# A two-layer mixer trunk on one core: three, and two, of the gate blocks computed beside the keys are handed out around the first attention units

## The chip, the cores and the metric

The kernel runs on one core of one Trainium2 chip. The metric is the time of one execution on the device in microseconds (us), as a median of runs. TensorE is called PE, its weight loads PEld, VectorE DVE, ScalarE ACT, GpSimd POOL and SyncE SP; SP issues all the transfers.

## The reference

Two layers (`DEPTH` = 2) over 1024 latent tokens of 1024 channels with 256 context tokens in front. All weights and activations are float32. Cut to what matters here:

```python
h = _rms(x) * (1.0 + scale) + shift                 # hc for the context tokens
fa, za, u, vs, zb, q, k, va, zc, g = _split_proj(h @ w_in[l])
q = _axial_rope(_qk(q, N_HEADS, q_norm_g[l]), row, col)      # 8 heads of 64
k = _axial_rope(_qk(k, N_KV_HEADS, k_norm_g[l]), row, col)   # 2 key heads
attn = _latent_attn(q, k, va, kc, vc, attn_sink[l])          # window +-128, plus all context keys
ya = _fourier(fa) * silu(za)
yb = _sgu(u, vs, w_s, b_s) * silu(zb)
yc = attn * silu(zc)
ga, gb, gc = split(sigmoid(g), 3)                            # the gates: 3 x 1024 channels
out = (ga * (ya @ w_pa) + gb * (yb @ w_pb) + gc * (yc @ w_pc)) @ w_out
x = x + gate * out
```

In layer 0 the context tokens go through the same (`out_c`), in layer 1 they only give keys and values.

## The kernel before

All matrix products are made of three float32r matmuls each (`mm3`, lines 229 to 231: high x high, high x low, low x high), so a weight tile `raw` is fetched (L209), cast to `whi` on ACT (L212), and the rest `wlo` is made by a subtraction on DVE (L213, called the split here). There are two `raw` buffers and five of `whi` and `wlo`. The tokens stand in three groups, "C" (256 of the context), "0" and "1" (512 latent ones each). A projection with channels on partitions (`proj_cm`) is a chain of 24 matmuls (8 slices of 128 input channels x 3) of 256 or 512 columns into one PSUM bank.

PSUM has eight banks, by tag: two `mm`, three `s`, two `pt`, one `o`. Nearly all chains of projections go into the two `mm` banks: keys and queries, and everything that is computed beside them.

`attention` first makes keys and values, one tile of 128 tokens after the other (the loop over `names`), then goes over the units: two query-head pairs of one token tile (of 128) each, first all tiles of key head 0, then of key head 1. Layer 0 has 40 units, the first four of them those of the context, layer 1 has 32. A unit needs its queries (`queries`, which keeps an `mm` bank from its chain through norm, rotary and transpose to L439), its scores (`scores`: L354 mask, L356, L357 and L363, reduces on DVE, exponentials on ACT, L379 on POOL) and its values (`values`: transposes L391, split on ACT and DVE L260 and L261, matmuls L398 and L399).

Other projections fill PE meanwhile. They are generators that yield the number of columns they have computed; a `Fill` runs them up to a given number. Two sets are used:

- `before_work`, handed out beside the keys as `early`. It computes gate blocks ahead (`ahead`): a block is the tanh of one 128-channel slice j of gate b (0, 1, 2) for one group. In layer 0 it is the first 12 blocks of the context group (`context_blocks(range(12))`), one after each key tile, and the rest at the end (`early.rest()`). In layer 1 it is the blocks (0, 1), (2, 1), (0, 2), (2, 2) of group "0", each in two halves of 256 columns (`part` = CTX), two halves after each key tile of group "1".
- `side_work`, handed out as `fills[0]` in the first half of the units and `fills[1]` in the second. The first yields the silu of the two `Z` and two `A` slices, and the rows `F`; how many columns come with each unit is `S["cost"]` over half the number of units.

The tanh of a gate block (L633) reads the bank and goes into a staging tile, `se` (two buffers of 256 columns) before the units, `st` (three of 512) from then on, and from there to memory (L634); `gates` reads it back much later (L545). A silu is a tanh on ACT (L551) and a multiplication on DVE (L552), which frees the bank.

The code does not fix the order on the engines: the instructions are recorded with `schedule_with_timeline_sim=True`, and the scheduler sorts them by its own estimate within what the dependences allow. A column number in `Fill` thus sets the order in which the instructions are recorded, which the scheduler starts from.

Of the kernel before, what the change touches and what calls it, by code (L numbers as in the profile page):

```python
# [66 lines left out]
def trunk_kernel(ctx: ExitStack, tc: tile.TileContext, a: dict, out: bass.AP):  # L67
# [343 lines left out]
    def attention(l, groups, sideA, sideB, xp, wkv, X, S):  # L411
# [48 lines left out]
        for ig, g in enumerate(names):  # L460
            if ig == 2:
                prepare(0)
                prepare(2)
            if X and ig < 2:
                modulate(l, names[ig + 1], X[names[ig + 1]], xp)
            g0, n = GROUPS[g]
            pk = bank("pt")
            for i in range(n // 128):
                t = g0 // 128 + i
                ib += 1  # L470
                p = bank("mm" if ib % 2 else "s")
                proj_tm(p, wt, H[g], i * 128)
                kf = qk_norm_rope(p, 2, 2, rope, None if g == "C" else t, np_)
                pv = p[:, 128:256].rearrange("p (g d) -> p g d", g=2)

                ACT.mul(vt[:, t, :, 0:64], pv, 0.5)
                DVE.scalar_tensor_tensor(vt[:, t, :, 64:128], pv, 0.5, vt[:, t, :, 0:64].bitcast(F32), ALU.mult, ALU.subtract)
                PE.transpose(pk[:, i * 128:(i + 1) * 128], kf[:, 0:128], ident)
                if "C" in groups:
                    early.upto(early.done + 1)  # L480
                elif ig == 2:
                    early.upto(early.done + CTX + 1)
            for kv in range(2):
                src = pk[kv * 64:(kv + 1) * 64, :n]
                hi = kk[0:64, kv, g0:g0 + n]
                ACT.copy(hi, src)
                DVE.tensor_tensor(kk[64:128, kv, g0:g0 + n], src, hi.bitcast(F32), ALU.subtract)
# [20 lines left out]
        def first(u):  # L508
            kv, g, t, pr = units[u]
            prepare(u)  # L510
            return scores(l, kv, pr, Q[kv, t], kk, local(u), ap)

        cur = first(0)
        nu = len(units)
        for u, (kv, g, t, pr) in enumerate(units):
            if u + 4 < nu:
                prepare(u + 4)
# [48 lines left out]
    def side_work(l, groups, S, st):  # L566

        ntok = sum(GROUPS[g][1] for g in groups)
        S["cost"] = [6 * ntok, 6 * ntok + 14 * CTX * ("C" in groups)]
        for g in groups:  # L570
            for j in range(4):
                stored(S, ("O" if j < 2 else "Z", j, g), GROUPS[g][1])
# [2 lines left out]
        def silus(name, col, js, keep=True):  # L575
            for j in js:
                w = w_cm(l, col + j * 128)
                for g in groups:
                    n = GROUPS[g][1]
                    p = bank("mm")  # L580
                    proj_cm(p, w, H[g], n)
                    s = staged(st, n)
                    silu2(s, p, n)
                    if name == "Y":
                        o = fetched(st, S["O", j, g], n, 2)
                        POOL.tensor_tensor(s, s, o, ALU.mult)
                    nc.sync.dma_start(S[name, j, g] if (name, j, g) in S else stored(S, (name, j, g), n), s)
                    yield n

        def gated_u():  # L590
            for j in range(2):
# [12 lines left out]
                    nc.sync.dma_start(stored(S, ("U", j, g), n), s)  # L604
                    yield 2 * n

        return ([silus("Z", C_ZC, (2, 3)), silus("A", C_ZA, (0, 1))] + [rows(l, groups, "F", C_FA, S, st)],
                [silus("Y", C_ZC, (0, 1)), gated_u()] + ([ahead(l, context_blocks(range(12, 24)), S, st), rows(l, ["C"], "V", C_VS, S, st)] if "C" in groups else []))

    def before_work(l, groups, S, st):  # L610

        if "C" in groups:
            return ahead(l, context_blocks(range(12)), S, st)
        return ahead(l, [(b, j, "0") for j in (1, 2) for b in (0, 2)], S, st, CTX)

    def few(gen, n):
        for _ in range(n):
# [498 lines left out]
```

## Time and profile before

| | before |
|---|---|
| median of 3 runs | 1968.52 us (1967.72 to 2089.09) |
| the profiled execution | 1967.06 us |
| its span, first to last instruction | 1965.3 us |
| PE busy | 1901.6 us, 97% |
| DVE, ACT, POOL busy | 1087.8, 799.5, 627.5 us |
| mean granted clock of PE | 0.994 |

The page's busy time of PE counts a matmul from its start to its modelled end; neighbours overlap, so a chain's length is read from the starts. An idle time stands in brackets behind the instruction that ended it, with the engine and the line that it waited for. The granted clock is 1.00 at 2.4 GHz and 0.50 at 1.2 GHz; a stretch between has both. The keys of layer 0 are made from about 45 to 145 us, its units run to about 500; in layer 1 the keys run to about 1180, the units to about 1490.

### The profile page before, as it was taken

The page shows a single profiled execution, that of the slowest core. Times are in us where ns is not written, and L with a number is a line of the kernel's source. Part 1 is how long each engine was busy: PE and PEld are TensorE (multiplying, and loading weights), DVE is VectorE, ACT ScalarE, POOL GpSimd, SP SyncE. Part 2 cuts the span into 40 slices and gives each one's busy share as a digit, 9 for nine tenths or more (in the row PEclk, how much of TensorE's full clock was granted, in tenths as well). Part 3 has the DMA queues.
Part 4 walks back from the last instruction along what each step waited for, and adds up shares of the span by engine and source line. Part 5 has one row for each costly group of instructions (what it writes and reads, how often), then busy time and mean ns, then how long its engine had stood idle before and what let it go on. Part 6 is the DMA issues. An engine that isn't in the chain of part 4 may idle for free.

```text
span 1965.3 us, 32941 instructions
## 1 busy us (share of the span) xinstructions
PE 1901.6 (97%) x11887; PEld 1688.0 (86%) x11887; DVE 1087.8 (55%) x2211; ACT 799.5 (41%) x2090; POOL 627.5 (32%) x1011
## 2 busy tenths in 40 slices
PE   7989999999999999999999989999999999999999
PEld 2888999999988887888899989899888888888898
DVE  4664665556655648766355455676665655622342
ACT  2653565445644422111243435565554443111320
POOL 1563344533331112211235543344432021211132
PEclk9999999999999999999999999999999999999999
DMA  8431121212565677654464312122134568632462
GB/s 309 119 99 64 50 68 54 79 44 84 163 188 164 188 226 227 171 174 141 148 229 165 108 47 75 54 61 82 34 91 149 158 186 270 191 106 82 134 225 87
DMA packets 281147, 259.91 MB, mean 132 GB/s; under 512 B 20824, under 2 KB 234520, under 8 KB 280984
## 3 DMA queue, kind: packets, MB, share of 16 engines
q1 hardware_dynamic: 280984, 257.80, 41.7%
q8 instruction: 94, 1.54, 0.3%
q14 instruction: 69, 0.57, 0.1%
HBM read 196.91 MB, written 60.83 MB: 131 GB/s over the span
## 4 chain that ended last, share of the span: by engine, by line
PE 82%; DMA 6%; DVE 5%; ACT 3%; issue 2%; POOL 2%; SPq 1%; POOLq 0%; DVEq 0%; ACTq 0%
PE mm L229 16%; PE mm L230 16%; PE mm L231 16%; PE s L230 6%; PE s L229 6%; PE s L231 6%; PE pt L391 3%; PE o L399 2%; PE o L398 2%; PE s L363 1%; PE s L356 1%; DVE wlo L213 1%; DMA raw<-in_w_in_dram 1%; PE s L166 1%; PE s L357 1%
## 5 line engine op out<-in xcount | busy, mean ns | idle before, releaser
L212 ACT CAST whi<-raw 128x1024 fp32r<-128x1024 f32 (+2 forms) x210 | 202.2, 966 | 393.7 <-PE s L230 144.6
L213 DVE TENSOR_TENSOR wlo<-raw,whi 128x1024 fp32r<-128x1024 f32 (+2 forms) x210 | 243.9, 1164 | 213.7 <-ACT whi L212 209.4
L229 PE MATMUL mm<-hh,whi 128*128 128x512 f32 (+1 forms) x768 | 296.2, 386 | 6.6 <-DVE st L552 4.2
L231 PE MATMUL mm<-hh,wlo 128*128 128x512 f32 (+1 forms) x768 | 294.2, 383 | 0.7 <-DVE wlo L213 0.7
L230 PE MATMUL mm<-hl,whi 128*128 128x512 f32 (+1 forms) x768 | 294.4, 383 | 0.0
L229 PE MATMUL mm<-whi,hh 128*128 128x256 f32 x832 | 239.7, 288 | 6.6 <-DVE qt L439 2.5
L231 PE MATMUL mm<-whi,hl 128*128 128x256 f32 x832 | 237.5, 285 | 0.0
L230 PE MATMUL mm<-wlo,hh 128*128 128x256 f32 x832 | 237.3, 285 | 0.0
L674 POOL TENSOR_TENSOR m<-m,tb 128x512 f32<-128x512 f32 x64 | 87.2, 1364 | 409.5 <-DVE tb L673 366.8
L229 PEld LDWEIGHTS mm<-hh,whi 128*128 128x128 f32 x768 | 145.2, 189 | 33.6 <-DVE st L552 5.1
L231 PEld LDWEIGHTS mm<-hh,wlo 128*128 128x128 f32 x768 | 145.1, 189 | 27.7 <-DVE wlo L213 0.9
L229 PEld LDWEIGHTS mm<-whi,hh 128*128 128x128 f32 x832 | 160.3, 193 | 9.0 <-issue 3.1
L230 PEld LDWEIGHTS mm<-hl,whi 128*128 128x128 f32 x768 | 145.3, 189 | 25.3
L231 PEld LDWEIGHTS mm<-whi,hl 128*128 128x128 f32 x832 | 160.5, 193 | 0.2 <-DVE hl L284 0.2
L230 PEld LDWEIGHTS mm<-wlo,hh 128*128 128x128 f32 x832 | 160.4, 193 | 0.2
L379 POOL TENSOR_SCALAR P<-P,rd 128x640 f32<-128x640 f32 (+2 forms) x144 | 110.7, 780 | 105.7 <-DVE rd L377 64.1
L230 PE MATMUL s<-hl,whi 128*128 128x512 f32 x352 | 137.5, 391 | 0.0
L229 PE MATMUL s<-hh,whi 128*128 128x512 f32 x352 | 137.4, 390 | 0.0
L231 PE MATMUL s<-hh,wlo 128*128 128x512 f32 x352 | 137.2, 390 | 0.0
L261 DVE TENSOR_TENSOR pl<-pt,ph 128x512 fp32r<-128x512 f32 (+1 forms) x184 | 112.4, 616 | 39.5 <-ACT ph L260 36.3
L260 ACT CAST ph<-pt 128x512 fp32r<-128x512 f32 (+1 forms) x184 | 96.1, 535 | 32.6 <-PE o L398 18.7
L196 DVE SCALAR_TENSOR_TENSOR aacc<-araw,scol,aacc 128x256 f32<-128x256 f32 x196 | 102.9, 558 | 5.2 <-DMA araw<-in_w_ada_dram 2.8
(303 smaller groups left out, 4637.1 us busy)
## 6 DMA issues: line engine op xcount, KB each, us to landing
raw<-in_w_in_dram SPq DMA_DIRECT2D x122, 512.0 KB, 4.1
araw<-in_w_ada_dram SPq DMA_DIRECT2D x48, 512.0 KB, 6.0
raw<-in_w_out_dram SPq DMA_DIRECT2D x40, 512.0 KB, 3.9
dP<-st SPq DMA_DIRECT2D x64, 256.0 KB, 2.7
lp<-dP SPq DMA_DIRECT2D x64, 256.0 KB, 4.2
x<-in_x_dram SPq DMA_DIRECT2D x16, 512.0 KB, 9.3
raw<-in_w_pc_dram SPq DMA_DIRECT2D x32, 256.0 KB, 2.9
dM<-m SPq DMA_DIRECT2D x32, 256.0 KB, 3.6
```

The lines of the kernel that those rows point to most:

```text
L196: DVE.scalar_tensor_tensor(acc[:, v, :], raws[k // 4][:, k % 4, :], sc, acc[:, v, :], ALU.mult, ALU.add)
L212: ACT.copy(hi, raw)
L213: DVE.tensor_tensor(lo, raw, hi.bitcast(F32), ALU.subtract)
L229: PE.matmul(o, lh, rh, start=start, stop=False)
L230: PE.matmul(o, lh, rl, start=False, stop=False)
L231: PE.matmul(o, ll, rh, start=False, stop=stop)
L260: ACT.copy(hi, src)
L261: DVE.tensor_tensor(lo, src, hi.bitcast(F32), ALU.subtract)
L379: POOL.tensor_scalar(P[hh][:, :nl + 256], P[hh][:, :nl + 256], rd[:, hh:hh + 1], 1.0, ALU.mult, ALU.mult)
L391: PE.transpose(b[:, (2 * i + hh) * 128:(2 * i + hh + 1) * 128], P[hh][:, (i0 + i) * 128:(i0 + i + 1) * 128], ident)
L398: PE.matmul(po, vs, ph[:, i * 256:(i + 1) * 256], start=(i0 + i == 0), stop=False)
L674: POOL.tensor_tensor(m, m, s, ALU.add)
```

## The change

Three of the context's gate blocks in layer 0 (10 to 12), and the two with j = 2 in layer 1, leave `before_work` and become the first generator of `fills[0]` (`lead`). One block is asked for before the first unit's scores (`fills[0].upto(1)`), and, in layer 0, one more behind them (`upto(CTX + 1)`); the next comes with the second unit. In layer 1 a held-back block is one chain of 512 columns instead of two of 256, and beside each key tile of group "1" stands one half block instead of two. `S["cost"]` grows by the columns that were added, so the share of each unit does too (layer 0: 7680 to 8448 columns over 20 units; layer 1: 6144 to 7168 over 16). The code below the change stands two or three lines lower: L551 and L552 become L553 and L554, L633 becomes L636.

```diff
--- before.py
+++ after.py
@@ -479,7 +479,7 @@
                 if "C" in groups:
                     early.upto(early.done + 1)
                 elif ig == 2:
-                    early.upto(early.done + CTX + 1)
+                    early.upto(early.done + 1)
             for kv in range(2):
                 src = pk[kv * 64:(kv + 1) * 64, :n]
                 hi = kk[0:64, kv, g0:g0 + n]
@@ -510,8 +510,10 @@
             prepare(u)
             return scores(l, kv, pr, Q[kv, t], kk, local(u), ap)
 
+        nu = len(units)
+        fills[0].upto(1)
         cur = first(0)
-        nu = len(units)
+        fills[0].upto(CTX + 1)
         for u, (kv, g, t, pr) in enumerate(units):
             if u + 4 < nu:
                 prepare(u + 4)
@@ -566,7 +568,7 @@
     def side_work(l, groups, S, st):
 
         ntok = sum(GROUPS[g][1] for g in groups)
-        S["cost"] = [6 * ntok, 6 * ntok + 14 * CTX * ("C" in groups)]
+        S["cost"] = [6 * ntok + (3 * CTX if "C" in groups else 1024), 6 * ntok + 14 * CTX * ("C" in groups)]
         for g in groups:
             for j in range(4):
                 stored(S, ("O" if j < 2 else "Z", j, g), GROUPS[g][1])
@@ -604,14 +606,15 @@
                     nc.sync.dma_start(stored(S, ("U", j, g), n), s)
                     yield 2 * n
 
-        return ([silus("Z", C_ZC, (2, 3)), silus("A", C_ZA, (0, 1))] + [rows(l, groups, "F", C_FA, S, st)],
+        lead = context_blocks(range(9, 12)) if "C" in groups else [(b, 2, "0") for b in (0, 2)]
+        return ([ahead(l, lead, S, st), silus("Z", C_ZC, (2, 3)), silus("A", C_ZA, (0, 1))] + [rows(l, groups, "F", C_FA, S, st)],
                 [silus("Y", C_ZC, (0, 1)), gated_u()] + ([ahead(l, context_blocks(range(12, 24)), S, st), rows(l, ["C"], "V", C_VS, S, st)] if "C" in groups else []))
 
     def before_work(l, groups, S, st):
 
         if "C" in groups:
-            return ahead(l, context_blocks(range(12)), S, st)
-        return ahead(l, [(b, j, "0") for j in (1, 2) for b in (0, 2)], S, st, CTX)
+            return ahead(l, context_blocks(range(9)), S, st)
+        return ahead(l, [(b, 1, "0") for b in (0, 2)], S, st, CTX)
 
     def few(gen, n):
         for _ in range(n):
```

What the change does to the order, at three places. Names are tiles with their number; a new number is a new tile. First PE in layer 0, behind the last key tiles. Before: the end of the chain `mm_1650` (silu of the context), four value matmuls of a context unit, and the beginning of `mm_1680` (silu of group "0") in the same bank:

```order
L230 MATMUL mm_1650<-hl1C_294,whi_1646 128x256
L231 MATMUL mm_1650<-hh1C_292,wlo_1647 128x256
L398 MATMUL o_1884<-ph_1890,vt_283 128x256
L399 MATMUL o_1884<-pl_1891,vt_283 128x256
L398 MATMUL o_1884<-ph_1890,vt_283 128x256
L399 MATMUL o_1884<-pl_1891,vt_283 128x256
L229 MATMUL mm_1680<-hh00_361,whi_1646 128x512
L230 MATMUL mm_1680<-hl00_363,whi_1646 128x512
```

Now, at the same number of matmuls: the end of the twelfth gate block `mm_1662`, transposes and values of two context units, and the silu of the context, `mm_1696`, in the gate's bank. The first latent queries (`mm_1531`, before `mm_1566`) have been projected just ahead of the gate and not behind it:

```order
L231 MATMUL mm_1662<-hh1C_292,wlo_1658 128x256
L391 MATMUL pt_1941<-ident_69,P_1812 128x128
L391 MATMUL pt_1941<-ident_69,P_1815 128x128
L391 MATMUL pt_1941<-ident_69,P_1812 128x128
L398 MATMUL o_1854<-ph_1860,vt_283 128x256
L391 MATMUL pt_1941<-ident_69,P_1815 128x128
L399 MATMUL o_1854<-pl_1861,vt_283 128x256
L398 MATMUL o_1854<-ph_1860,vt_283 128x256
L399 MATMUL o_1854<-pl_1861,vt_283 128x256
L229 MATMUL mm_1696<-hh0C_291,whi_1692 128x256
L230 MATMUL mm_1696<-hl0C_293,whi_1692 128x256
```

The gate's chain moved behind the query. Next DVE in layer 0, a little later, where the silu of group "0" or "1" is emptied beside the first latent scores. Before: `mm_1854`, with the weight split `wlo_2864` and two reduces ahead of L552:

```order
L328 TENSOR_TENSOR qf_1810<-qf_1810,ta_1815 128x256
L358 TENSOR_REDUCE red_1904<-s_1909 128x1
L365 TENSOR_REDUCE red_1904<-s_1914 128x2
L213 TENSOR_TENSOR wlo_2864<-raw_2861,whi_2863 128x1024
L358 TENSOR_REDUCE red_1904<-s_1924 128x1
L552 SCALAR_TENSOR_TENSOR st_1879<-ta_1880,mm_1854 128x512
L367 TENSOR_REDUCE nm_1907<-red_1904 128x1
L439 TENSOR_TENSOR qt_1821<-mm_1776,qt_1821 64x2x128
```

Now: the chain in the same place is `mm_1824`, and the same split stands nine rows behind its emptying instruction:

```order
L328 TENSOR_TENSOR qf_1780<-qf_1780,ta_1785 128x256
L358 TENSOR_REDUCE red_1874<-s_1879 128x1
L554 SCALAR_TENSOR_TENSOR st_1849<-ta_1850,mm_1824 128x512
L365 TENSOR_REDUCE red_1874<-s_1884 128x2
L358 TENSOR_REDUCE red_1874<-s_1894 128x1
L439 TENSOR_TENSOR qt_1791<-mm_1746,qt_1791 64x2x128
L367 TENSOR_REDUCE nm_1877<-red_1874 128x1 x2
L439 TENSOR_TENSOR qt_1791<-mm_1746,qt_1791 64x2x128
L376 TENSOR_REDUCE rd_1905<-den_1876 128x2
L377 RECIPROCAL rd_1905<-rd_1905 128x2
L358 TENSOR_REDUCE red_2012<-s_2017 128x1
L213 TENSOR_TENSOR wlo_2864<-raw_2861,whi_2863 128x1024
```

So one reduce stands ahead of the emptying instruction, and the split ahead of the next one's. Last PE in layer 1, between the gate blocks beside the keys. Before: the end of the first block's second half (`mm_13464`), a transpose of a key tile, scores, and both halves of the second block (`mm_13543`, `mm_13571`):

```order
L231 MATMUL mm_13464<-hh10_12297,wlo_13432 128x256
L478 MATMUL pt_13384<-ident_69,qf_13524 128x128
L363 MATMUL s_13852<-kk_12987,qt_13325 128x256 x4
L229 MATMUL mm_13543<-hh00_12296,whi_13538 128x256
L230 MATMUL mm_13543<-hl00_12298,whi_13538 128x256
L229 MATMUL mm_13571<-hh00_12296,whi_13538 128x256
L230 MATMUL mm_13571<-hl00_12298,whi_13538 128x256
L231 MATMUL mm_13543<-hh00_12296,wlo_13539 128x256
```

Now: the projection of the last key tile (`mm_13536`, before `mm_13599` and behind the second block), then the scores and the second block's first half (`mm_13587`):

```order
L229 MATMUL mm_13536<-whi_13004,hh11_12889 128x256
L230 MATMUL mm_13536<-wlo_13005,hh11_12889 128x256
L231 MATMUL mm_13536<-whi_13004,hl11_12891 128x256
L363 MATMUL s_13761<-kk_12987,qt_13325 128x256 x4
L229 MATMUL mm_13587<-hh00_12296,whi_13582 128x256
L230 MATMUL mm_13587<-hl00_12298,whi_13582 128x256
L231 MATMUL mm_13587<-hh00_12296,wlo_13583 128x256
```

The key tile's chain of 24 matmuls stands between the two blocks. The second half (`mm_13659`) follows in the key tile's bank, then the first held-back block, `mm_13723`, of 512 columns.

## Rows read from the trace of the kernel before

**Rows 1.** The page: span, busy time of the engines, and the casts of weights

```profile
span 1965.3 us, 32941 instructions
PE 1901.6 (97%) x11887; PEld 1688.0 (86%) x11887; DVE 1087.8 (55%) x2211; ACT 799.5 (41%) x2090; POOL 627.5 (32%) x1011
...
L212 ACT CAST whi<-raw 128x1024 fp32r<-128x1024 f32 (+2 forms) x210 | 202.2, 966 | 393.7 <-PE s L230 144.6
```

**Rows 2.** Busy time of PE by stretch: its length, busy time (instructions), granted clock

```profile
core 0: us, PE busy (x), PEclk, DMA share, GB/s
142.30:181.40 39.10, 34.61 (x230) 0.96 0.30 93
181.40:330.00 148.60, 147.27 (x1100) 1.00 0.16 48
1142.00:1177.00 35.00, 28.28 (x198) 0.90 0.21 61
1177.00:1500.00 323.00, 315.57 (x2138) 1.00 0.23 72
```

**Rows 3.** Chain of waits, layer 0: start, length, what it went through

```profile
159.40 0.60 ACT ta L551
160.03 0.70 DVE st L552
...
170.73 1.21 DVE wlo L213
171.94 0.33 DVE red L358
```

**Rows 4.** Timeline of PE, layer 0: start, length, instruction, idle time before it

```profile
153.39 0.50 PE L229 MATMUL mm<-hh,whi 128*128 128x512 f32 x1 [1.28 <-DVE st L552]
...
160.77 0.39 PE L229 MATMUL mm<-whi,hh 128*128 128x256 f32 x1 [0.94 <-DVE st L552]
...
172.93 0.39 PE L229 MATMUL mm<-hh0C,whi 128*128 128x256 f32 x1 [2.26 <-DVE st L552]
```

**Rows 5.** PE by stretch as in rows 2: chains after a wait, and two undisturbed ones

```profile
153.40:159.00 5.60, 5.60 (x26) 1.00 0.26 73
...
172.93:177.39 4.46, 4.46 (x24) 0.62 0.54 176
177.98:180.85 2.87, 2.87 (x24) 1.00 0.15 49
1209.02:1214.57 5.55, 5.55 (x24) 1.00 0.18 64
```

**Rows 6.** Timeline of PE, layer 1, the last key tiles

```profile
1145.09 0.38 PE L356 MATMUL s<-kk,qt 128*128 128x256 f32 x1 [2.38 <-POOL qt L441]
...
1152.44 0.35 PE L229 MATMUL mm<-hh,whi 128*128 128x256 f32 x1 [1.90 <-DVE qt L439]
...
1161.03 0.39 PE L229 MATMUL mm<-hh,whi 128*128 128x256 f32 x1 [0.44 <-ACT whi L212]
...
1162.51 0.39 PE L231 MATMUL mm<-hh,wlo 128*128 128x256 f32 x1 [0.69 <-DVE wlo L213]
...
1175.86 0.65 PE L478 MATMUL pt<-ident,qf 128*128 128x128 f32 x2 [0.89 <-DVE qf L328]
```

**Rows 7.** Timelines of PE and DVE: last matmuls of two key tiles, what frees them

```profile
1150.15 0.28 PE L231 MATMUL mm<-whi,hl 128*128 128x256 f32 x1
...
1153.47 0.28 DVE L477 SCALAR_TENSOR_TENSOR vt<-mm,vt 128x128 fp32r<-128x128 f32 x1
...
1170.87 0.28 PE L231 MATMUL mm<-whi,hl 128*128 128x256 f32 x1
...
1175.44 0.69 DVE L328 TENSOR_TENSOR qf<-qf,ta 128x128 f32<-128x128 f32 x2
...
1176.65 1.21 DVE L213 TENSOR_TENSOR wlo<-raw,whi 128x1024 fp32r<-128x1024 f32 x1
1177.79 0.28 DVE L477 SCALAR_TENSOR_TENSOR vt<-mm,vt 128x128 fp32r<-128x128 f32 x1
```

## The prediction, made before the result was known

> **What bounds the kernel.** I read the page's first section, then busy time by stage, then the waits of TensorE (PE) in the stages that the change touches, then the chains behind those waits. PE is busy 97% of a span of 1965.3 us [rows 1], so a change saves time only where PE stands idle or runs at the lower of its two clock levels. By stage [rows 2] that is nearly all in two places: 142.3 to 181.4 us (first units of the attention in layer 0, 39.10 us with 34.61 busy, granted clock 0.96) and 1142 to 1177 us (keys of token group "1" in layer 1, 35.00 with 28.28 busy, 0.90). The stretches behind them have 1.33 us idle in 148.6 and 7.43 in 323. Idle time and clock together make 4.5 + 6.7 us and 0.04 x 39.1 + 0.10 x 35.0 = 5.1 us: some 16 us are within reach, 0.8% of the whole.
>
> In the first place PE waits three times, 1.28, 0.94 and 2.26 us, always to begin a chain of 24 matmuls, always for DVE at L552 [rows 4]. L552 empties an `mm` bank, of which there are two. In [rows 3] the hand-over is seen bare: tanh on ACT from 159.40 (0.60), L552 from 160.03 (0.70), PE again at 160.77, 1.37 us in all for a 512-column silu chain. At 170 us it is longer, since a weight split (`wlo`, 1.21 us) and a reduce stand ahead of L552 on DVE. After this 2.26 us wait the granted clock falls: the next chain takes 4.46 us at a mean grant of 0.62, where 24 matmuls of the same width take 2.87 at 1.00 [rows 5]; 1.59 us lost. After the wait of 1.28 none is seen (1.00 from 153.40 to 159.00). Together the place loses 4.48 + 1.59 = 6.1 us.
>
> In the second place five waits stand in [rows 6]: 2.38 for POOL's copy of the first query tile, 1.90 for the bank of a query (L439), 0.44 and 0.69 for the weights of a gate block, 0.89 for a normed key tile.
>
> **The change, part by part.** *Layer 0.* Of the twelve gate blocks, three are held back. The order shows that ten and eleven stand where they stood: PE's program is the same up to 142.3 us, so the waits before that stay. What moves is the twelfth block, now behind the query projection of the first latent tile, so queries, and with them all that follows, come one chain earlier. Three hand-overs of banks are left that are as tight. I count the matmuls between a bank's last chain and its next, at 2.87/24 = 0.12 us [rows 5]. Before: 4, 4 and 11 of them (0.5, 0.5, 1.3 us) against waits of 1.28, 0.94, 2.26. Now: 8 (1.0 us), 6 (0.7) and 11 (1.3). The first empties a gate, one tanh and no L552: the 0.60 of [rows 3] at most, hidden by 1.0. The second empties a 256-column silu: at most 1.37 - 0.7, I take 0.5. The third is a 512-column silu with one reduce (0.33 in [rows 3] at 171.94) ahead of it and the weight split now behind it: 1.37 + 0.33 - 1.3, I take 0.4. No wait is near 2 us, so I expect no fall of the clock. Sum: 4.48 + 1.59 - 0.9 = **-5.2 us**. Bounds: -6.1 with no wait left; +0 if the three cost what the old ones do.
>
> *Layer 1.* Four halves of 256 columns (tokens of group "0" for blocks 0 and 2, j = 2) become two chains of 512: 4 x 2.87 = 11.48 against 2 x 5.55 = 11.10 [rows 5], -0.4. The second gate block no longer follows the first; a key tile's chain stands between them (2.87 us), in which its cast and split (0.97 us on the mean of [rows 1], and 1.2 in [rows 3]) fit: the waits of 0.44 and 0.69 go, -1.1. The transposes of 433 (`qf` to `mm`) stand two matmuls later, which puts off the bank of the 1.90 us wait by 0.2. Then the key tile itself: before, its last matmul started at 1170.87 and its transpose could begin at 1175.86 [rows 6, 7], 5.0 us later. Now 24 + 7 matmuls, 3.7 us, and the last one's own 0.12 lie between: a wait of 1.1 instead of 0.89, +0.2. Behind it a gate chain needs that tile's bank, which L477 frees: in [rows 7] 3.6 us after the chain for one tile (1150.15 to 1153.75) and 7.2 us for the other (1170.87 to 1178.07), whose L477 stood behind a weight split. In the new order L477 stands ahead of the split; cover with the wait is 5.0 us, so between 0 and 2.2; I take 0.3, nearer to the tile without a split ahead. Queued on PE behind this chain are the first held-back block and the scores of the next unit, and ACT and DVE wait for those scores. Sum: **-0.8 us**, bounds -2.4 and +3.
>
> *What is costed at nothing.* The held-back blocks' weights come by the same number of transfers on SP; a fetch now and then stands behind a store, and the chains have a query or scores ahead of them. They are staged in `st` (three buffers), which nothing else uses that early, in place of `se` (two). In layer 1 ACT runs two tanh of 512 in place of four of 256, and SP issues two stores for four; neither engine is near its limit (41% for ACT, [rows 1]). POOL's order in the first units changes only with the units. The fill per unit rises from 384 to 422 columns in layer 0 and from 384 to 448 in layer 1: work that was done earlier, now inside units that have 1.3 and 7.4 us idle in all [rows 2], so it can fill little and, unless it comes late, cost little. For the reshuffled order in those stretches I allow 2 us either way.
>
> **The sum.** -5.2 - 0.8 = -6.0 us. The profiled execution took 1967.06 us with its span of 1965.3; that gives 1961. The median of the runs is 1968.52, 1.5 above it; from there it is 1962.5. I predict **1962 us**, its own range 1958 to 1966.
>
> **The rivals.**
> (a) *The waits only move.* Two `mm` banks, chains of 24 matmuls and queries that hold a bank for many microseconds are what they were; a hand-over that is now covered leaves another bare. For it: three tight hand-overs remain of three, and the stretch from 1177 has its 7.4 us with full fills. Against it: the split is behind the silu now. Then the time stays at 1967 to 1968.
>
> (b) *The clock falls at shorter waits.* PE's clock stayed at the upper level, 2.4 GHz, after the wait of 1.28 [rows 4, 5]; if waits of that size or less were enough in another position, each of the three left would bring a chain at the lower level, 1.2 GHz, for part of it, at 1.59 us: 6.0 - 3 x 1.59 = 1.2 saved, 1967. The Trainium skill, "TensorE: Matmul & The Clock Gate", section "A second HAM failure mode: psum-queue depth-cycling", tells of a kernel that cycles through PSUM banks and in which frequent micro-idles between groups of matmuls make the clock swing between its levels; by that rule the kernel would come out here at about 1967. The trace does not bear it out after the wait of 1.28 us; after that of 2.26 it does.
>
> (c) *Slower: the four tight hand-overs cost what the worst row does.* Place: the three in layer 0 and the key tile's bank in layer 1. Price: 2.26 + 1.59 = 3.9 us each, 15.4, against what goes: 6.1, 1.1 and 0.4. That is 7.8 us slower, 1976. It decides from 7.6/4 = 1.9 us each. For it: L477's 7.2 us in [rows 7]. Against it: it needs DVE to be late four times, and in the new order no split stands on DVE between a chain's end and the instruction that empties its bank.
>
> (d) *Nothing changes, since the order around the units was found by the scheduler anyway.* It did leave blocks ten and eleven in place; but the query did move. This has the time of (a) and is counted there.
>
> **How the numbers follow.** Forecast 0.62; (a) with (d) 0.22; (b) 0.08; (c) 0.08. The range 1957.5 to 1968 takes in the bounds of -6.1 and -2.4 with 2 us of drift below, and (a) and (b) above; it leaves out (c) and some tails. Two per cent, about what a measurement of this kernel can tell from no change, is 39 us, more than twice all that is within reach. So faster by over 2% gets 0.01, within 2% 0.97, slower by over 2% 0.02.
>
> **What would show it.** Right: in the profile after, PE's waits for the silu's DVE line (L554 now) between 142 and 181 us sum to about 1 us in place of 4.5, no half-clock stretch begins near 173 us, and the stretch has a clock of 1.00; in layer 1 the waits for `whi` and `wlo` near 1161 us are gone while those of 2.38 and about 2 us, and with them a clock below 1 in that stretch, are still there. Wrong: a wait over 1.9 us for an `mm` bank with a fall of the clock behind it, a wait of 2 us for L477 near 1167 us, or more than 10 us idle in the second stretch of either layer.

## The result, and the profile after

The changed kernel takes 1955.99 us (median of 6 runs, 1952.97 to 1958.51) against 1967.81 us for the kernel before beside it: a ratio of 0.9946, 95% interval 0.9933 to 0.9959, or 10.6 us (8.1 to 13.2) less. One run of the kernel before, of 2089.09 us, was a slow one and is not in the ratio. Two later measurements of the same kernel gave 6.9 (4.3 to 9.2) and 7.9 us (5.5 to 10.2); the mean of the three is 8.5. The time stays within 2%, as forecast, but the change is clear of zero: with an interval 0.26% wide a measurement of this kernel tells far less from no change than the 2% that the prediction named. The forecast of 1962 was too high, and the first median lies 2 us below the forecast's own range (1958 to 1966) and 1.5 below the wider one (1957.5 to 1968).

The page after, as [rows 1]:

```profile
span 1954.1 us, 32830 instructions
PE 1899.2 (97%) x11839; PEld 1686.4 (86%) x11839; DVE 1090.1 (56%) x2211; ACT 799.2 (41%) x2088; POOL 633.2 (32%) x1011
```

PE by stretch after, as [rows 2]: first units and following units of layer 0, then the keys and the units of layer 1 (each 9 us earlier than in the rows of before, since everything is by then):

```profile
142.30:181.40 39.10, 38.51 (x265) 1.00 0.32 95
181.40:330.00 148.60, 148.56 (x1122) 1.00 0.19 56
1133.00:1168.00 35.00, 30.04 (x187) 0.85 0.25 73
1168.00:1491.00 323.00, 314.76 (x2101) 0.99 0.23 70
```

In the first stretch PE has 0.59 us idle in place of 4.49 [rows 2], at clock 1.00; in the second 0.04 in place of 1.33. In layer 1 the keys are busier (30.04 against 28.28), but at 0.85 in place of 0.90, and the units idle 8.2 us in place of 7.4. PE's waits in these places, as [rows 4, 6]:

```profile
148.90 0.39 PE L229 MATMUL mm<-hh0C,whi 128*128 128x256 f32 x1 [0.38 <-ACT st L636]
...
1136.02 0.58 PE L356 MATMUL s<-kk,qt 128*128 128x256 f32 x1 [2.38 <-POOL qt L441]
...
1144.30 0.35 PE L229 MATMUL mm<-hh,whi 128*128 128x256 f32 x1 [1.86 <-DVE qt L439]
...
1158.84 0.33 PE L478 MATMUL pt<-ident,qf 128*128 128x128 f32 x1 [0.27 <-DVE qf L328]
1159.39 0.35 PE L229 MATMUL mm<-hh,whi 128*128 128x256 f32 x1 [0.22 <-DVE vt L477]
...
1376.45 0.50 PE L229 MATMUL mm<-hh,whi 128*128 128x512 f32 x1 [2.02 <-DVE st L554]
```

The three waits of layer 0 are gone, one of 0.38 (a gate's tanh) is new. In layer 1 those for `whi` and `wlo` are gone, 2.38 and 1.86 stand. The last row's wait was there before, with the same 2.02 us; PE of the kernel before:

```profile
1387.02 0.50 PE L229 MATMUL mm<-hh,whi 128*128 128x512 f32 x1 [2.02 <-DVE st L552]
```

What was not there is the half clock behind it. Stretches of PE after, this one first, then the two of layer 1's keys:

```profile
1377.61:1381.03 3.42, 3.42 (x10) 0.50 0.22 81
1135.27:1142.10 6.83, 6.08 (x28) 0.50 0.01 2
1145.51:1148.92 3.41, 3.41 (x18) 0.50 0.00 0
```

### The profile page after: what moved, and what is told of

It is laid out like the page before. It is cut to its first block, busy times and chain, and to the rows that moved or that the text cites. A ratio compares the mean times of both kernels' runs of the same rounds, so it can differ in the third digit from the quotient of the medians.

```text
span 1954.1 us, 32830 instructions
## 1 busy us (share of the span) xinstructions
PE 1899.2 (97%) x11839; PEld 1686.4 (86%) x11839; DVE 1090.1 (56%) x2211; ACT 799.2 (41%) x2088; POOL 633.2 (32%) x1011
## 4 chain that ended last, share of the span: by engine, by line
PE 84%; DMA 5%; DVE 4%; ACT 2%; issue 2%; POOL 1%; SPq 1%; POOLq 0%; DVEq 0%; ACTq 0%
PE mm L229 17%; PE mm L230 16%; PE mm L231 16%; PE s L230 6%; PE s L229 6%; PE s L231 6%; PE pt L391 3%; PE o L399 2%; PE o L398 2%; PE s L363 1%; PE s L356 1%; DMA lt<-dT 1%; PE s L166 1%; PE s L357 1%; DMA araw<-in_w_ada_dram 1%
## 5 line engine op out<-in xcount | busy, mean ns | idle before, releaser
L212 ACT CAST whi<-raw 128x1024 fp32r<-128x1024 f32 (+2 forms) x210 | 202.2, 966 | 388.1 <-PE s L230 144.0
L213 DVE TENSOR_TENSOR wlo<-raw,whi 128x1024 fp32r<-128x1024 f32 (+2 forms) x210 | 245.0, 1170 | 204.2 <-ACT whi L212 198.9
L261 DVE TENSOR_TENSOR pl<-pt,ph 128x512 fp32r<-128x512 f32 (+1 forms) x184 | 111.8, 615 | 24.4 <-ACT ph L260 22.4
```

Source lines behind the costliest of these rows:

```text
L212: ACT.copy(hi, raw)
L213: DVE.tensor_tensor(lo, raw, hi.bitcast(F32), ALU.subtract)
L261: DVE.tensor_tensor(lo, src, hi.bitcast(F32), ALU.subtract)
```

## The experiments

All kernels compute the whole output. Gains in us are the ratio and its interval applied to 1966.1, the median of the kernel before in 34 runs (1965.9 to 1966.5 in the other batches; 1967.8 for the first result). Lengths of stages are differences between the starts of the same matmuls in each trace: layer 0 from a chain at 121.94 us (in before) to a projection behind its attention at 493.94; layer 1 from 1140.79 (its keys) to the first projection behind its attention at 1497.23. The rest is the span less both. Each diff is shortened; a two-line `if` stands on one line.

**The kernel before and after again, and the two edits alone.**

From the changed kernel to layer 0 alone (`e1`), the edit of layer 1 taken out; `e2` does the reverse with the other branch of the same lines:

```diff
-                    early.upto(early.done + 1)
+                    early.upto(early.done + CTX + 1)
-        fills[0].upto(1)
+        if "C" in groups: fills[0].upto(1)
-        fills[0].upto(CTX + 1)
+        if "C" in groups: fills[0].upto(CTX + 1)
-        S["cost"] = [6 * ntok + (3 * CTX if "C" in groups else 1024), 6 * ntok + 14 * CTX * ("C" in groups)]
+        S["cost"] = [6 * ntok + (3 * CTX if "C" in groups else 0), 6 * ntok + 14 * CTX * ("C" in groups)]
-        lead = context_blocks(range(9, 12)) if "C" in groups else [(b, 2, "0") for b in (0, 2)]
+        lead = context_blocks(range(9, 12)) if "C" in groups else []
-        return ahead(l, [(b, 1, "0") for b in (0, 2)], S, st, CTX)
+        return ahead(l, [(b, j, "0") for j in (1, 2) for b in (0, 2)], S, st, CTX)
```

Layer 0 alone. 

> Only the edit of layer 0 (blocks 10 to 12 held back, the two calls ahead of the loop, the larger cost); layer 1 as before. Theory A (the gain is made where the order changed: bank hand-overs in the first units): PE's waits for L554 between 142 and 181 us sum to at most 0.5 us in place of 4.48, no half-clock stretch near 173, and the kernel is 6 to 8 us faster than before. Theory B (about 4 of the 10 to 12 us are made by a shift of everything behind, in parts of the program that are the same): the two layers' edits alone do not add up to the whole; this one gives 6 to 8 and the other nothing like 4. Theory C (the prediction's sum): 5.2 us.

Layer 1 alone. 

> Only the edit of layer 1 (two blocks held back, one half block beside each key tile, cost + 1024); layer 0 as before. Theory A: the waits of 0.44 and 0.69 for whi and wlo near 1161 us are gone, those of 2.38 and 1.90 stand, the half clock near 1146 to 1157 stays; 1 to 3 us faster than before, and with the run of the layer 0 edit alone this adds up to the whole, 10 to 12. Theory B: 0 to 1 us faster, the sum of both stays 3 us or more below the whole. Theory C: 0.8 us.

The kernel before. 

> The kernel before, unchanged but for a comment: what two executions of one program differ by. Theory A: its trace differs from the first one outside the change's places by as much as the traces of before and after do there (0.8 us at the start, about 1.3 in the middle, 2.4 after 1494 us, and a half-clock stretch more or less behind the same wait near 1377 to 1387 us), and its waits of 1.28, 0.94 and 2.26 us in layer 0 stand. Theory B: outside the change's places the two traces of before agree within 1 us, so the 2.4 us after 1494 us come from the change. Time ratio to before 1.000 within 0.1%.

The changed kernel, second and third time. 

> The changed kernel, unchanged but for a comment: a second profile and a closer time. The layer 0 edit alone measured 7.9 us (5.5 to 10.2), the layer 1 edit alone 0.4. Theory A (gain made where the order changed, the two edits add up, the rest of the first comparison is scatter): 7 to 10 us faster than before, the profile has the one wait of about 0.38 near 149 us between 142 and 181, and outside the change's places it differs from the first profile of after by 1 to 3 us (start, waits at 1006, evictions after 1494). Theory B (both edits together give more than their sum): 10 to 13 us faster. Half clock behind the wait of 2.0 us near 1377 us: there in the two profiles with the layer 1 edit so far, in none of the four without; if it belongs to the edit it stands here too.

> The changed kernel once more, unchanged but for a comment, beside kernels that differ by one split. Two measurements so far: 10.6 (8.1 to 13.2) and 6.9 us (4.3 to 9.2) faster than before. Theory A (the gain is that of layer 0, 7 to 8 us, and layer 1 adds nothing): 6.5 to 9.5 us. Theory B (both edits together give more than their sum): 10 or more. If A holds the half clock behind the 2.0 us wait near 1380 us stands again, as in the three profiles with the layer 1 edit.

| kernel | faster than before, us | layer 0 stage | layer 1 stage | rest of the span |
|---|---|---|---|---|
| before, first profile | | 372.00 | 356.44 | 1236.9 |
| before again (e3) | 0.6 (-1.4 to 2.8) | 371.86 | 355.14 | 1232.8 |
| layer 1 alone (e2) | 0.4 (-1.2 to 2.2) | 372.01 | 355.97 | 1236.1 |
| layer 0 alone (e1) | 7.9 (5.5 to 10.2) | 365.02 | 355.04 | 1234.1 |
| after, first profile | 10.6 (8.1 to 13.2) | 364.95 | 356.63 | 1232.5 |
| after again (e5) | 6.9 (4.3 to 9.2) | 365.38 | 356.67 | 1238.7 |
| after, third (e13) | 7.9 (5.5 to 10.2) | 364.93 | 354.16 | 1232.7 |

The layer 0 stage is the same within 0.5 us in these profiles wherever its program is the same, and 6.9 us shorter with its edit. The layer 1 stage does not change by more than its scatter. The rest, in which all these kernels have the same PE order, spreads over 6 us: `e5` has 1.92 us of wait for `whi` (L212) at 1001 us, where the first profile of after has none, and its first transfers and late evictions shift likewise. The first comparison of traces (11.2 us of span) was 7.0 of layer 0, -0.2 of layer 1 and 4.4 of this scatter. So the gain is layer 0's, and the whole is no more than the sum of its parts within the intervals. The changed kernel's second time, 6.9, is just under theory A's 7 to 10, its third within 6.5 to 9.5. For the layer 1 edit theory A's 1 to 3 us was missed: 0.4, not clear of zero, is theory B's. Waits in the places of the change repeat to 0.1 us, as before again shows against [rows 4]:

```profile
153.10 0.50 PE L229 MATMUL mm<-hh,whi 128*128 128x512 f32 x1 [1.29 <-DVE st L552]
160.48 0.39 PE L229 MATMUL mm<-whi,hh 128*128 128x256 f32 x1 [0.94 <-DVE st L552]
...
172.63 0.39 PE L229 MATMUL mm<-hh0C,whi 128*128 128x256 f32 x1 [2.26 <-DVE st L552]
```

The chain behind the last, as a stretch:

```profile
172.63:177.10 4.47, 4.47 (x24) 0.62 0.55 176
```

**How many blocks are held back (layer 0 alone).** As `e1`, with another number:

```diff
-        lead = context_blocks(range(9, 12)) if "C" in groups else []
+        lead = context_blocks(range(6, 12)) if "C" in groups else []
-            return ahead(l, context_blocks(range(9)), S, st)
+            return ahead(l, context_blocks(range(6)), S, st)
```

for six; 11, 10 and 8 in place of 6 for one, two and four, and `S["cost"]` with as many times CTX. With one block there is no second call.

> Layer 0 only, one block held back (the twelfth) in place of three, cost + CTX. The order leaves the query ahead of the silu, as in the kernel before: hand-overs of an mm bank with 0.36, 0.48 and 1.28 us of matmuls between (before: 0.48, 0.48, 1.28) and the split ahead of the third L552 as before. Theory A (the cover of the hand-overs and the place of the split make the gain): waits of about 1.4, 0.94 and 2.26 us and the half clock near 173 stand; 0 us, at most 1 us either way in the stretch. Rival (holding back work at all, or the larger share of the units, makes it): a third or more of the gain of the layer 0 edit, 2.5 us or more.

> Layer 0 only, two blocks held back, cost + 2 x CTX. In the order the two silus with 0.48 us of matmuls between still stand, the third tight hand-over has 5 us. Theory A (the time follows the covers of the hand-overs): waits of 1.28 and 0.94 us stand, that of 2.26 and the half clock near 173 go: 3 to 4.5 us faster than before, between one block (0.2 measured) and three (7.9). Rival (three is a threshold of another kind): as one block, 0 to 1.

> Layer 0 only, four blocks held back, cost + 4 x CTX. In the order the hand-overs have 0.65 and 0.74 us (gates, which need a tanh alone) and 1.02 us (a silu of 256 columns). Six blocks gave 0: their first units had 2.4 us less idle, but the end of the keys, 134 to 142 us, had 1.90 and 0.70 us of waits and a half clock that were not there before. Theory A (what is taken from the end of the keys is missed there as soon as the queries and scores are not ready): no wait above 0.6 us in 142 to 181, and a part of the waits of six blocks between 130 and 142, so 4 to 8 us faster. Rival (any block beyond three costs a chain's 2.9 us at the keys): 4 to 5.5.

> Layer 0 only, six blocks held back in place of three, cost + 6 x CTX. In the order no hand-over of a silu is under 2.3 us of matmuls; the gates have 0.87 to 1.5. Theory A: no wait above 0.6 us for a bank and no half clock in the first units, so as fast as the layer 0 edit alone, 6 to 9 us faster than before; beside the keys four chains fewer leave key tiles bare, which may cost up to 2 us there. Rival (three is what counts, since more work in the units pushes queries and scores later): 0 to 5 us faster, with new waits of scores or queries between 142 and 500 us.

| held back | faster than before, us | layer 0 stage less 371.9 |
|---|---|---|
| one | 0.2 (-1.8 to 2.2) | -1.3 |
| two | 5.7 (3.5 to 7.9) | -4.4 |
| three | 7.9 (5.5 to 10.2) | -6.9 |
| four | 4.9 (2.9 to 6.9) | -4.8 |
| six | -0.2 (-2.6 to 2.0) | +0.8 |

One block moves no query and leaves the three waits where they were (1.30, 0.94, 2.26). Two leave the first two, as expected, and in the place of the third 0.35 and 0.65 (L554 is L556 in these kernels); the time is better than the 3 to 4.5 us expected, the stage is not:

```profile
153.47 0.50 PE L229 MATMUL mm<-hh,whi 128*128 128x512 f32 x1 [1.28 <-DVE st L556]
160.85 0.39 PE L229 MATMUL mm<-whi,hh 128*128 128x256 f32 x1 [0.94 <-DVE st L556]
173.16 0.38 PE L398 MATMUL o<-ph,vt 128*128 128x256 f32 x1 [0.35 <-ACT ph L260]
174.20 0.38 PE L229 MATMUL mm<-whi,hh 128*128 128x256 f32 x1 [0.65 <-DVE st L556]
```

Four have new ones, 0.75, 0.61 and 1.09 us, all for `mm` banks. The order's 0.65 to 1.02 us of matmuls between chains told the places but not the sizes, and the bound of 0.6 in the expectation did not hold. The time of 4.9 fits theory A and its rival alike, but the place fits neither: between 130 and 142 us no wait is new, and the new ones stand in the first units. Six blocks are the surprise against theory A. PE of six blocks, waits; its stretches; and the first two of these stretches in before again:

```profile
134.03 0.38 PE L363 MATMUL s<-kk,qt 128*128 128x256 f32 x1 [0.70 <-ACT P L371]
141.02 0.63 PE L391 MATMUL pt<-ident,P 128*128 128x128 f32 x4 [1.90 <-POOL qf L320]
```

```profile
100.00:142.00 42.00, 33.28 (x255) 0.96 0.26 73
142.00:181.00 39.00, 36.88 (x253) 0.96 0.30 90
142.12:145.53 3.41, 3.41 (x18) 0.50 0.34 89
```

```profile
100.00:142.00 42.00, 35.76 (x281) 0.96 0.32 93
142.00:181.00 39.00, 34.51 (x229) 0.96 0.31 93
```

The first units gain 2.37 us of busy time, the end of the keys loses 2.48, and the half clock that stood near 173 stands at 142. With six blocks gone from there PE waits for probabilities (L371) and for POOL, where it had gates to compute before; in the units one bank keeps it waiting for 0.92 us (162.01), over the 0.6 expected. This is the prediction's rival (a), "the waits only move", at another dose.

**The share of the units alone.** In the kernel before:

```diff
-        S["cost"] = [6 * ntok, 6 * ntok + 14 * CTX * ("C" in groups)]
+        S["cost"] = [6 * ntok + (3 * CTX if "C" in groups else 0), 6 * ntok + 14 * CTX * ("C" in groups)]
```

> The kernel before with the larger cost alone in layer 0 (8448 columns over 20 units in place of 7680), nothing held back. In the order two tight hand-overs stay (0.48 us of matmuls each, silus of 256 and of 512 columns), the third has 3.9 us. Theory A: waits of 1.28 and 0.94 stand, that of 2.26 and its half clock go: 2.5 to 4 us faster than before (the fill runs out a unit earlier, which may cost up to 1.5). Rival (the gain needs blocks held back): 0 us, or slower by the fill that is missing in the last unit.

1.8 us faster (-0.6 to 4.1), its stage 3.1 shorter. The first two waits stand (1.29, 0.94), that of 2.26 is 0.29; new ones of 0.80 and 0.86 us come at 204 and 329. So the larger share alone also moves the chains' places, and takes away the largest wait with its half clock; its timed gain is not clear of zero, and less than half of the stage's 6.9 us is gone.

**Three held back, nothing asked for ahead of the loop.** From `e1`:

```diff
-        if "C" in groups: fills[0].upto(1)
         cur = first(0)
-        if "C" in groups: fills[0].upto(CTX + 1)
```

> Layer 0 only, three blocks held back and the larger cost, but nothing asked for ahead of the loop over the units: the fill hands the blocks out with the units. In the order a query takes the bank with 0.12 us of matmuls behind a gate, and two gates follow each other with 0.13 us in the other bank; the silus have 3.8 us. Theory A: waits of 0.3 to 0.9 us for these two banks, none of 1.28, 0.94 or 2.26, no half clock at 173: 5 to 7.5 us faster. Rival (the calls that place blocks around the first scores are what makes the gain): scores wait at the beginning of the units and the gain is 0 to 3.

7.1 us faster (4.3 to 9.8), its stage 5.7 shorter: one gate waits 1.18 us at 142.56, more than the 0.9 expected. The two calls are worth about 1.1 us in the stage, too little for the times to tell.

**One weight split moved to POOL.** `granule` gets an engine for L213; for one slice it is POOL:

```diff
-                w = w_cm(l, col + j * 128)
+                w = w_cm(l, col + j * 128, POOL if l == 0 and name == "A" and j == 1 else None)
-                wz = w_cm(l, C_ZB + j * 128)
+                wz = w_cm(l, C_ZB + j * 128, POOL if l == 1 and j == 1 else None)
```

The first line is that of layer 0 (e4, e16), the second that of layer 1 (e12, e14, e15, e16): the split ahead of the emptying instruction at 1376 us. DVE of the changed kernel there:

```profile
1373.46 1.22 DVE L213 TENSOR_TENSOR wlo<-raw,whi 128x1024 fp32r<-128x1024 f32 x1
1374.59 0.69 DVE L365 TENSOR_REDUCE red<-s 128x2 f32<-128x512 f32 x1
1375.19 0.15 DVE L376 TENSOR_REDUCE rd<-den 128x2 f32<-128x6 f32 x1
1375.26 0.55 DVE L358 TENSOR_REDUCE red<-s 128x1 f32<-128x384 f32 x1
1375.72 0.68 DVE L554 SCALAR_TENSOR_TENSOR st<-ta,mm 128x512 f32<-128x512 f32 x1
```

Layer 0's split, in the kernel before. 

> The kernel before with one weight split (wlo of the last A slice in layer 0, 1.21 us on DVE at 170.73) done on POOL, so that it no longer stands ahead of L552 there; PE's order stays but for a few rows. It tells whether the split made the wait of 2.26 us and the half clock behind it. Theory A: the wait of 2.26 shrinks by about 1.2 to near 1.0, no half clock follows, so 2.6 to 2.8 us faster than before (unless PE then waits for wlo, which POOL may give later: at most 1 to 2 us back). Rival (the wait is set by the chain of tanh and L552 alone, or the clock falls by itself): the wait stays above 1.9 us or the half clock stands without it; 0 to 1.2 us faster.

Layer 1's split, in the kernel before. 

> The kernel before with only the second wz's split of layer 1 on POOL; PE's order is the same row for row. In the two profiles of before the wait there was 2.02 us and no half clock followed. Theory A: the wait falls to 0.9, all later starts are 1.1 us earlier, 1 to 1.5 us faster than before. Rival (the half clock follows this wait in a part of the executions in the kernel before too, though not in the profiled ones): 1.5 to 2.7 us. Second rival (POOL's own work is late behind a split of 2.4 us): 0.

Both, in the kernel before. 

> The kernel before with both splits on POOL, that of layer 0 and that of layer 1. The split of layer 0 alone took 2.7 us out of the profile (the wait of 2.26 fell to 1.12 and the half clock went) and yet measured 0.3 us (-1.6 to 2.4). Theory A (the profile is right and the timed runs scattered): 3.5 to 5 us faster than before. Rival (what the split frees in layer 0 is lost again in other executions, by half clocks elsewhere): as the split of layer 1 alone, within 1 us.

Layer 1's split, with the layer 0 edit alone. 

> The layer 0 edit alone, layer 1 as before, but the second wz's split of layer 1 on POOL. PE's order is that of the layer 0 edit alone. The changed kernel with the same split moved was 11.8 us faster than before. Theory A (moving the split is worth 1.1 us of wait, and 1.5 of half clock where there is one; the layer 1 edit is worth the 2 us of its removed waits when no half clock takes them back): 8.5 to 10 us faster than before, 2 to 3 less than with the layer 1 edit. Rival (the layer 1 edit is worth nothing even then): as with it, 11 to 13.

Layer 1's split, in the changed kernel. 

> The changed kernel with one weight split of layer 1 (wlo of the second wz, 1.22 us on DVE at 1378.84 in the second profile of after) done on POOL, so that it no longer stands ahead of L554 there, and the wait of 2.0 us near 1377 to 1382 with the half clock behind it shrinks. PE's order changes in a few places behind. Theory A (a split ahead of the instruction that empties a bank lengthens the wait, and the wait of 2 us brings the half clock in the changed kernel): the wait is 0.8 to 1.0, no half clock near 1380, 2 to 3 us faster than the changed kernel, so 8.5 to 12 faster than before. Rival (the half clock in that place has nothing to do with the wait, or POOL is late with the split): a half clock stays in that place, 0 to 1 us faster than the changed kernel, 6 to 9 than before.

| kernel | faster than before, us | wait at the place of the split |
|---|---|---|
| before, split of layer 0 (e4) | 0.4 (-1.6 to 2.4) | 2.26 to 1.12 |
| before, split of layer 1 (e15) | 3.3 (1.4 to 5.1) | 2.02 to 0.91 |
| before, both (e16) | 3.9 (1.8 to 6.1) | 2.26 to 1.12, 2.02 to 0.90 |
| layer 0 edit, split of layer 1 (e14) | 8.3 (5.5 to 11.0) | 2.02 to 0.90 |
| changed kernel, split of layer 1 (e12) | 11.8 (8.8 to 14.7) | 2.02 to 0.90 |

In each trace the wait falls by 1.1 us, nearly the split's length (1.2 us on DVE). The kernel before with layer 0's split on POOL, PE's wait and the chain behind it:

```profile
173.11 0.39 PE L229 MATMUL mm<-hh0C,whi 128*128 128x256 f32 x1 [1.12 <-DVE st L552]
```

```profile
173.11:175.98 2.87, 2.87 (x24) 1.00 0.48 143
```

The changed kernel with layer 1's, the same two views:

```profile
1372.25 0.50 PE L229 MATMUL mm<-hh,whi 128*128 128x512 f32 x1 [0.90 <-DVE st L554]
```

```profile
1372.25:1376.00 3.75, 3.75 (x16) 1.00 0.54 173
```

So the split ahead made these waits 1.1 us longer, and behind what is left, 0.9 and 1.1 us, no half clock follows in these traces. What it is worth in the time is clear of zero for one of the two places only. Layer 1's split gave 3.3 us (1.4 to 5.1) where the traces have 1.1. The first rival, that the half clock follows this wait in some executions of the kernel before too, is not enough as far as the traces show: of ten profiles with this wait and without the layer 1 edit one has it, about 0.2 us in the mean. Layer 0's gave 0.4, and 3.9 less 3.3 is 0.6, where the stage is 3.1 and 2.5 us shorter in the two profiles. The 3.9 fits theory A and its rival alike. Both profiles have two half-clock pieces at layer 1's keys, as the first profile of before has and before again has not; no run shows that the missing gain goes there. Where it goes stays open.

`e12` has the lowest median, 1953.73 us, but its interval overlaps those of the changed kernel. In part this is a rescheduled order: with the split gone the scheduler moved PE rows behind it too, and a wait of 1.67 us for L370 at 1417.93 became 1.11. Its layer 1 stage is 351.29 us against 354.16 to 356.67 of the changed kernel. It has no half clock near 1377 us, which all three profiles of that kernel have, and at the keys one piece of it where two of those have three. Without the layer 1 edit the same split gave 8.3; the intervals overlap, so that the edit is worth 2 to 3 us once the 2.0 us wait is shorter is not shown.

## Why the prediction was right and wrong

The time fell below the range. The mechanism was right and the sum too small: two terms of layer 0 were mis-sized, and the starting value was 2.4 us too high.

*The bound and the places.* The places are right: all the gain that repeats lies in the place of the three `mm` hand-overs and the stretch behind it. The bound of -6.1 for layer 0 was too tight: the stage is 6.9 us shorter.

*Layer 0, -5.2.* The mechanism holds: query and gate changed places, the split went behind the emptying instruction, 4.48 us of waits and the 1.59 of half clock went. The step that failed is the size of two terms of its sum. The first is "0.9 left", which was 0.38, and not where it was looked for: the gate's hand-over, taken as hidden, waits 0.38, and the two silus, taken at 0.5 and 0.4, wait less than 0.2 each. The gate's tanh stands behind a weight cast on ACT that the prediction did not count; ACT of the changed kernel:

```profile
147.51 1.05 ACT L212 CAST whi<-raw 128x1024 fp32r<-128x1024 f32 x1 [1.10 <-PE mm L230]
148.47 0.38 ACT L636 ACTIVATE st<-mm 128x256 f32<-128x256 f32 x1
```

Between the silus' chains PE is busy for longer than 0.12 us a matmul: the six take from 151.87 to 152.96 us, 1.1 in place of 0.7, the eleven from 161.40 to 162.97, 1.6 in place of 1.3. And the reduce ahead of the second silu's L554, which the prediction added, runs beside the tanh:

```profile
161.60 0.60 ACT L553 ACTIVATE ta<-mm 128x512 f32<-128x512 f32 x1 [4.11 <-PE mm L231]
161.84 0.42 DVE L358 TENSOR_REDUCE red<-s 128x1 f32<-128x256 f32 x1 [0.85 <-PE s L357]
162.23 0.69 DVE L554 SCALAR_TENSOR_TENSOR st<-ta,mm 128x512 f32<-128x512 f32 x1
```

The second term is the 1.33 us idle of the stretch behind, which the prediction put at nothing in its sum ("can fill little", with 2 us either way allowed). It went too: two waits of the kernel before are not in the changed one, and the one of 0.24 at 337 us stood before at 345. PE of the kernel before:

```profile
241.17 0.39 PE L399 MATMUL o<-pl,vt 128*128 128x256 f32 x1 [0.82 <-DVE pl L261]
...
266.91 0.39 PE L229 MATMUL mm<-whi,hh0C 128*128 128x256 f32 x1 [0.46 <-DVE st L552]
```

In all 4.10 + 1.59 + 1.28 = 7.0, against 6.9 measured in the stage. The kernel with one block held back separates the second term: its three waits stand, of 0.82 is left 0.35 and the 0.46 is gone, and its stage is 1.3 us shorter, too little for its time to tell. Of the first term the times do not settle each part: `e4` took 1.14 of wait and the 1.59 of half clock out of its trace, and its time moved by 0.4 (-1.6 to 2.4).

*Layer 1, -0.8.* The sum is within the scatter (0.4 timed, 0.3 between the mean stages of four profiles with the edit and the ten without it and with the same split; neither is clear of zero), by other terms. The waits for `whi` and `wlo` went, and the feared hand-over behind L477 cost 0.22. But against them stand 1.67 for L370 where 1.11 was, 1.02 for L261 where 0.35 was, and the half clock after the 2.02 us wait, 1.5 us. (The first two stand in all three profiles of the changed kernel; with layer 1's edit alone the wait for L370 is 1.11, as before, and that for L261 0.09.) This is the sign that the prediction listed as "wrong": a wait over 1.9 us for an `mm` bank with a fall of the clock. It looked for it only where the order changed; it came 200 us later, at a wait that had been there.

*The sum.* From 1968.52, the median of three runs, it took 1962.5. With more runs the kernel before has 1966.1. So of the 4.9 us between 1962.5 and the mean result (1966.1 - 8.5 = 1957.6), 2.4 are the starting value, 1.7 layer 0, and 0.8 is within the intervals. The two microseconds of drift that the range allowed were too few for the rest of the program alone, which spreads by 6 between single executions. How far the first result fell below the range is in part chance: the medians of the same kernel are 1955.99, 1959.79 and 1956.51.

*The rivals.* (a) is refuted for three blocks; with four and six other waits do stand in the place of those that went. (b), that the clock falls at shorter waits, does not occur in layer 0's units: none follows 0.38, 0.75, 0.94, 1.09, 1.12 or 1.28. In the places of the change falls are seen only behind waits of 1.79 to 2.38 us. Elsewhere in the same program they are seen behind shorter ones: at 762 us in `e11` behind 0.82 us and eight matmuls of one column (L200), at 1006 us in the kernel with one block held back behind 0.97 and 0.76 us whose ends are 1.3 us apart. In the kernel before 1.59 and 0.76 us stand at the latter place with no fall. The Trainium skill, "TensorE: Matmul & The Clock Gate", section "A second HAM failure mode: psum-queue depth-cycling", puts such a swinging clock down to frequent short idles of PE between groups of matmuls. For the places of the change the traces give that no support; the two falls elsewhere could be of that kind. (c) priced four hand-overs at 3.9 us each; they cost 0.38, under 0.2 twice, and 0.22. (d) fell with (a): the query did move, and the time with it.

## What to carry to other kernels

Where PE waits for a bank, count the matmuls between the bank's last chain and its next, and look at what stands on the emptying engine ahead of the emptying instruction: a weight split there lengthened two waits by 1.1 us, and swapping a query with a gate's chain made the waits go. Held-back work has a best amount (0.2, 5.7, 7.9, 4.9 and -0.2 us for one, two, three, four and six blocks): with four new hand-overs are bare, with six the work is missed where it was taken from. For gains under 1%, profile the same program twice and compare stages between the same instructions: the stage of layer 0 repeats to 0.5 us where the span moves by 5.5 (two profiles of before) and 8.9 us (three of after).

## What the runs showed of the hardware

The length of a wait alone does not decide whether the clock falls. In the 18 traces half clock begins at the wait of 2.55 us near 112 us and at that of 2.38 us near 1140 us every time, at that of 2.26 us near 173 us in all five that have it, at one of 2.5 us near 120 us in four of 18, and at that of 1.8 to 2.0 us behind the 2.38 in 11 of 18. After the 2.02 us wait near 1380 us the clock fell to half in all four profiles with layer 1's edit and this wait, and in one (four blocks held back) of the ten that have the wait without the edit; why the edit matters there no run shows. The chain behind it in before again, and in the changed kernel's second profile:

```profile
1383.00:1387.00 4.00, 4.00 (x17) 1.00 0.37 142
```

```profile
1382.52:1385.93 3.41, 3.41 (x10) 0.50 0.22 84
```

The keys of layer 1 had one, two or three pieces of 3.4 us at half clock in profiles with the same PE rows there, and the piece at 120 us, which makes 17 matmuls take 3.5 us in place of 2.1, stood in four profiles and not in the others. Such pieces, and waits for `whi` and `wlo` at 1001 to 1008 us, make 3.7 of the 5.5 us by which the spans of the two profiles of before differ: 2.35 of waits that one has and the other has not, and 1.3 in layer 1's keys.
